# Retention values: copied from their bank at once, and scaled and turned two at a time

## The chip, the cores and the metric

The kernel runs on one core of a Trainium2 chip. The metric is the device time of one execution in microseconds (us), lower is better. The core has a matrix engine (TensorE, PE), a vector engine (VectorE, DVE), a scalar engine (ScalarE, ACT), GpSimd (POOL) and a queue that issues transfers (SyncE, SP). They run side by side and wait for one another only through semaphores. Matrix results land in PSUM, eight banks of 512 fp32 numbers per partition; a bank can be given to the next result when the last reader of the old one is through.

## The reference

The reference is one layer of a decoder: 512 tokens, width 1024, fp32. A normalised x is projected by one wide matrix to the inputs of two branches, a retention and a dilated attention, and to their two gates; the branches are merged and followed by an MLP and a gated embedding. The change concerns the retention alone. Its output y of head h (four heads, 256 wide) is found in four chunks of 128 tokens, then normalised over the 256 columns, gated and projected:

```python
y = retention_chunkwise(rq, rk, rv)
y = rmsnorm(y, ret_gn.reshape(RET_HEADS, RET_DV)).reshape(B, S, RET_V)
ret_branch = (jax.nn.silu(rg) * y) @ w_ret_out
```

With y the 128x256 result of one chunk and one head (called a value below), what is needed of it is the mean of its squares per token, the power -1/2 of that, the product of y, this factor and the gate G, and the transpose of the product, since the next matrix product wants columns.

## The kernel before, in words

All large products run on PE with each fp32 operand split in a high and a low part, three matmuls each (lines 260 to 262). A weight tile of 128x1024 is loaded (raw), its high part is copied out by ACT (whi, line 248) and its low part is the difference taken by DVE (wlo, line 249). Six raw tiles and four pairs of split tiles exist, so ACT and DVE work a few tiles ahead of PE and wait for PE to free them. Some weight tiles are sums of others: POOL issues transfers that add to a tile (line 226), and DVE adds tiles (line 224).

The heads have little work and are strewn into the large products. `later` puts a step on a list with a lag, and `tick`, called after every few matmuls of a product, takes steps off the list when their lag is over. Steps thus get their place in the written program from ticks; the framework's scheduler then sets the order of each engine's instructions. Each engine works its own queue strictly in that order.

The retention works in two pairs of heads. For each pair, a product of seven parts (`seven_products`, numbered m in the code) makes the pair's v and G. The steps of the pair's two heads (`ret_head`) are put on the list after that and run inside the next large product: those of heads 0 and 1 inside the product for v and G of heads 2 and 3, those of heads 2 and 3 inside the first of two gate products (`gates`, called in `mix`). The steps of a head are: scores (rs, line 978; masked by DVE to rsT, line 981), three states (kv, line 986; the first copied by ACT, line 989, the others summed by DVE to st, line 991), and four values (ry, lines 998 and 1000).

A value before the change goes this way. ACT takes its squares with their sum (line 1002). DVE makes the mean from the sum (v, line 325, in `rstd`), POOL takes the power (r, line 326), and DVE multiplies the bank's content by r and G into the tile At (line 1004). Three ticks later PE turns At in two transposes into another bank (pt, line 1010), and ACT copies the two halves with the norm's gains into A (line 1013). Steps up to line 1004 are written in one piece.

All small results, rs, kv, ry and pt, take their bank from one pool of four; part 2 of a seven-part product holds two of these four (pa) from its first half to its second. The second head of a pair runs in that time, so its scores, states and values share the other two. With G come its own DVE steps (lines 957, 959) and a sigmoid on ACT (line 958); with a gate product come sums and products on DVE (g, lines 1043 and 1045) and a sigmoid (line 1058). The framework gives a bank's next tile to the place that comes free first, so that the scores of the second head get the bank of the first head's third value, and the state behind them that of its fourth.

Of the kernel before, what the change touches and what calls it, by code (L numbers as in the profile page):

```python
# [13 lines left out]
AF = mybir.ActivationFunctionType  # L14
ALU = mybir.AluOpType
AX = mybir.AxisListType

P = 128
S = 512
D = 1024  # L20
NT = S // P
# [59 lines left out]
class Block:  # L81
# [292 lines left out]
    def turn(self, x, out, goff):  # L374

        ps = self.bank("pt")
        for k in range(4):
            self.nc.tensor.transpose(ps[:, k * P : (k + 1) * P], x[:, k * P : (k + 1) * P], self.ident)
        g = self.gcol[:, goff : goff + 4].unsqueeze(2).to_broadcast([P, 4, P])
        self.nc.vector.tensor_tensor(out, ps.rearrange("p (k t) -> p k t", k=4), g, op=ALU.mult)  # L380
# [586 lines left out]
    def ret_head(self, h, qk, v, G, inner, eps, A):  # L967
        nc = self.nc
        qT, kT, kd = qk
        c = slice((h % 2) * 256, (h % 2) * 256 + 256)  # L970
        hs = slice(h * HD, (h + 1) * HD)
        sT, st = [], []

        def scores():
            sc = self.bank("rs")
            for n in range(NT):
                i = slice(n * P, (n + 1) * P)
                nc.tensor.matmul(sc[:, i], kT[:, h, i], qT[:, h, i], start=True, stop=True)
            t = self.tmp("rsT")
            v4 = lambda ap: ap.rearrange("p (n i) -> p n i", n=NT)  # L980
            nc.vector.tensor_tensor(v4(t), v4(sc), inner.unsqueeze(1).to_broadcast([P, NT, P]), op=ALU.mult)
            sT.append(t)

        def state(n):
            ps = self.bank("kv")[:, :256]
            nc.tensor.matmul(ps, kd[:, n, hs], v[:, n, c], start=True, stop=True)
            s = self.tmp("st")[:, :256]
            if n == 0:
                nc.scalar.activation(s, ps, AF.Copy)
            else:  # L990
                nc.vector.tensor_tensor(s, st[-1], ps, op=ALU.add)
            st.append(s)

        def values(i):
            y = self.bank("ry")[:, :256]
            ss = self.small(1, "ss")
            r = slice(i * P, (i + 1) * P)
            nc.tensor.matmul(y, sT[0][:, r], v[:, i, c], start=True, stop=i == 0)
            if i:
                nc.tensor.matmul(y, qT[:, h, r], st[i - 1], start=False, stop=True)  # L1000
            At = self.tmp("At")
            nc.scalar.activation(At[:, 256:], y, AF.Square, accum_out=ss)
            r = self.rstd(ss, 1, 256, eps[:, i, h : h + 1])
            nc.vector.scalar_tensor_tensor(At[:, :256], y, r, G[:, i, c], op0=ALU.mult, op1=ALU.mult)
            self.later(3, lambda: turn(At, i), ("A", h, i))

        def turn(At, i):
            ps = self.bank("pt")
            for k in range(2):
                nc.tensor.transpose(ps[:, k * P : (k + 1) * P], At[:, k * P : (k + 1) * P], self.ident)  # L1010
            for k in range(2):
                g = self.gcol[:, 8 + 2 * h + k : 9 + 2 * h + k]
                nc.scalar.activation(A[h // 2][:, 2 * (h % 2) + k, i * P : (i + 1) * P], ps[:, k * P : (k + 1) * P],
                                     AF.Copy, scale=g)

        self.later(0, scores)
        for n in range(NT - 1):
            self.later(0, lambda n=n: state(n))
        for i in range(NT):
            self.later(2, lambda i=i: values(i))  # L1020
# [31 lines left out]
    def mix(self, A, O):  # L1052
        nc = self.nc
# [8 lines left out]

        self.gates(16, spill, "cb")
        for h in range(H):
            for i in range(NT):
                self.force(("A", h, i))
        O = self.merged_split(O)
        G = [self.big("Ga") for _ in range(2)]
        part = lambda kk: G[kk % 4 // 2][:, kk % 2 + kk // 4 * 2]
# [344 lines left out]
```

## Time and profile before

| | before |
| --- | --- |
| median of 3 runs | 968.77 us (967.72 to 969.59) |
| profiled execution, its own time | 968.49 us |
| its span, first to last instruction | 966.7 us |
| granted clock of PE | 1.00 |
| PE busy | 956.3 us, 5404 instructions |
| DVE busy | 721.1 us, 1029 instructions |
| ACT busy | 533.3 us, 1027 instructions |
| POOL busy | 146.4 us, 136 instructions |

In a timeline row stand start, duration, engine, line, operation, what is written from what, shapes, the number of merged instructions, and in brackets how long the engine was idle before it and what ended that. In a row of a group, the numbers behind the bar are busy us, mean ns of one, and idle us before them with what ended most of it. PEld are the weight loads of PE, which run beside its matmuls. The time of one execution is some 1.8 us more than the span. The two pairs of heads run between 330 and 440 us.

### The profile page before, as it was taken

How to read it: one execution, taken by the hardware profiler on the slowest of the kernel's cores; microseconds unless marked ns; L12 is line 12 of the kernel's file. 1: busy time of each engine (PE TensorE's matmuls, PEld its weight loads, DVE VectorE, ACT ScalarE, POOL GpSimd, SP SyncE). 2: the span in 40 equal slices, each digit the busy share in tenths (PEclk: the TensorE clock that was granted, in tenths of full speed). 3: DMA queues.
4: the chain of work that ended last, by engine and by line, in shares of the span. 5: the costliest groups of instructions: out<-in, count | busy, mean ns of one | idle time of the engine just before them, and what ended most of it. 6: DMA issues, size and time to landing. Idle time of an engine off the chain costs nothing.

```text
span 966.7 us, 14352 instructions
## 1 busy us (share of the span) xinstructions
PE 956.3 (99%) x5404; PEld 843.1 (87%) x5404; DVE 721.1 (75%) x1029; ACT 533.3 (55%) x1027; POOL 146.4 (15%) x136
## 2 busy tenths in 40 slices
PE   9999999999999999999999999999999999999998
PEld 6888899889888878899988888998998998898886
DVE  7857665775969957476856879799589679769953
ACT  6535344546636646467713445893585476468551
POOL 0310220210001021313002210211202202111100
PEclk9999999999999999999999999999999999999999
DMA  9832123234348564759757686968959868886911
GB/s 335 264 99 73 61 87 87 66 105 154 105 110 204 172 126 131 132 152 222 209 177 218 153 184 185 213 156 211 190 164 199 196 179 158 224 187 150 276 64 55
DMA packets 87189, 155.50 MB, mean 161 GB/s; under 512 B 6816, under 2 KB 18768, under 8 KB 87120
## 3 DMA queue, kind: packets, MB, share of 16 engines
q1 hardware_dynamic: 66304, 114.72, 36.4%
q0 software_dynamic: 20672, 39.85, 24.8%
q8 instruction: 42, 0.69, 0.3%
q14 instruction: 27, 0.22, 0.1%
q10 hardware_dynamic: 144, 0.02, 0.0%
HBM read 148.24 MB, written 6.33 MB: 160 GB/s over the span
## 4 chain that ended last, share of the span: by engine, by line
PE 90%; issue 4%; DVE 3%; POOL 2%; DMA 1%; ACT 1%; SPq 0%; POOLq 0%; DVEq 0%; ACTq 0%
PE pg L260 26%; PE pg L261 26%; PE pg L262 25%; PE pa L262 2%; PE pa L261 2%; PE pa L260 2%; PE po L734 1%; PE ph L587 1%; POOL r L326 1%; DVE wlo L249 1%; PE sc L711 1%; PE pe L679 1%; POOL raw L226 1%; DMA raw<-in_w_down 1%; PE sc L717 1%
## 5 line engine op out<-in xcount | busy, mean ns | idle before, releaser
L249 DVE TENSOR_TENSOR wlo<-raw,whi 128x1024 fp32r<-128x1024 f32 (+1 forms) x246 | 292.5, 1197 | 111.8 <-ACT whi L248 110.6
L248 ACT ACTIVATE whi<-raw 128x1024 fp32r<-128x1024 f32 (+1 forms) x245 | 253.4, 1039 | 213.0 <-PE pg L262 99.4
L260 PE MATMUL pg<-whi,hh 128*128 128x512 f32 x344 | 137.8, 402 | 0.0
L262 PE MATMUL pg<-whi,hl 128*128 128x512 f32 x344 | 134.7, 391 | 0.0
L261 PE MATMUL pg<-wlo,hh 128*128 128x512 f32 x344 | 134.5, 391 | 0.0
L260 PE MATMUL pg<-f,whi 128*128 128x256 f32 x384 | 108.9, 284 | 0.5 <-DVE r L1222 0.5
L261 PE MATMUL pg<-f,whi 128*128 128x256 f32 x384 | 108.7, 283 | 0.0
L262 PE MATMUL pg<-f,wlo 128*128 128x256 f32 x384 | 108.6, 283 | 0.0
L262 PEld LDWEIGHTS pg<-whi,hl 128*128 128x128 f32 x344 | 72.4, 210 | 11.2
L260 PEld LDWEIGHTS pg<-whi,hh 128*128 128x128 f32 x344 | 72.4, 211 | 10.4 <-ACT whi L248 0.3
L261 PEld LDWEIGHTS pg<-wlo,hh 128*128 128x128 f32 x344 | 72.6, 211 | 10.0
L260 PE MATMUL pg<-whi,f 128*128 128x512 f32 x192 | 75.4, 393 | 0.0
L261 PE MATMUL pg<-wlo,f 128*128 128x512 f32 x192 | 74.8, 390 | 0.0
L262 PE MATMUL pg<-whi,f 128*128 128x512 f32 x192 | 74.8, 389 | 0.0
L260 PEld LDWEIGHTS pg<-f,whi 128*128 128x128 f32 x384 | 73.7, 192 | 1.0 <-ACT r L1224 0.7
L261 PEld LDWEIGHTS pg<-f,whi 128*128 128x128 f32 x384 | 73.7, 192 | 0.2
L262 PEld LDWEIGHTS pg<-f,wlo 128*128 128x128 f32 x384 | 73.7, 192 | 0.0
L642 POOL TENSOR_TENSOR r<-v,mhalf 128x4 f32<-128x4 f32 x24 | 30.0, 1253 | 153.5 <-DVE v L641 150.6
L226 POOL DMA_DIRECT2D raw<-in_w_down x24 | 29.0, 1216 | 141.1 <-DVE wlo L249 112.4
L226 POOL DMA_DIRECT2D raw<-in_w_in x20 | 24.4, 1218 | 170.0 <-DVE wlo L249 157.6
L226 POOL DMA_DIRECT2D raw<-in_w_up x24 | 29.0, 1210 | 134.4 <-DVE wlo L249 129.1
L260 PEld LDWEIGHTS pg<-whi,f 128*128 128x128 f32 x192 | 36.1, 188 | 8.1 <-issue 0.4
(274 smaller groups left out, 2186.3 us busy)
## 6 DMA issues: line engine op xcount, KB each, us to landing
raw<-in_w_in SPq DMA_DIRECT2D x72, 512.0 KB, 3.9
raw<-in_w_up SPq DMA_DIRECT2D x32, 512.0 KB, 4.7
raw<-in_w_down SPq DMA_DIRECT2D x32, 512.0 KB, 4.7
raw<-in_w_up POOLq DMA_DIRECT2D x24, 512.0 KB, 7.5
raw<-in_w_down POOLq DMA_DIRECT2D x24, 512.0 KB, 6.1
raw<-in_w_in POOLq DMA_DIRECT2D x20, 512.0 KB, 6.4
x<-in_x SPq DMA_DIRECT2D x8, 512.0 KB, 8.3
raw<-in_w_ret_out SPq DMA_DIRECT2D x8, 512.0 KB, 4.1
```

What stands on the lines that cost most here:

```text
L226: self.nc.gpsimd.dma_start(raw, self.chained[i].rearrange("(k p) n -> p k n", p=P), accum_op=ALU.add)
L248: self.pin(nc.scalar.activation(R(hi[:, i]), raw[:, i], AF.Copy))
L249: nc.vector.tensor_tensor(R(lo[:, i]), raw[:, i], hi[:, i], op=ALU.subtract)
L260: t.matmul(ps, sh, mh, start=first, stop=False, skip_group_check=more)
L261: t.matmul(ps, sh, ml, start=False, stop=False, skip_group_check=more)
L262: t.matmul(ps, sl, mh, start=False, stop=last, skip_group_check=more)
L326: self.nc.gpsimd.tensor_tensor(r, v, self.mhalf[:, :w], op=ALU.pow)
L587: self.nc.tensor.transpose(ps[:, t * P : (t + 1) * P], rots[t][:, h * HD : (h + 1) * HD], self.ident)
L642: nc.gpsimd.tensor_tensor(r, v, self.mhalf[:, :H], op=ALU.pow)
L679: self.nc.tensor.transpose(ps[:, k * P : (k + 1) * P], e[:, k * P : (k + 1) * P], self.ident)
L711: nc.tensor.matmul(sc[:, h * P : (h + 1) * P], qT[:, h, rs], kT[:, h, rs], start=True, stop=True)
L717: nc.tensor.matmul(sc[:, h * 256 : (h + 1) * 256], qT[:, 2 * hp + h, rs], kT[:, 2 * hp + h, (r - 1) * P : (r + 1) * P], start=True, stop=True)
```

## The change

A value leaves its bank by ACT alone: a copy to At, then the squares, written back into the bank, with their sum. Two values share one At (256 columns each) and one small tile each for sums, means and powers. When the second of the two is there, `means` makes both means in one DVE instruction and both powers in one POOL instruction; `scale`, two ticks later, multiplies each half of At in place by its power and by G on DVE; `turn`, three ticks later, turns both values by four transposes into one bank, and ACT copies them to A in two instructions of 128x256. What waits for A at the end of `mix` asks for two keys per head instead of four.

```diff
         def values(i):
             y = self.bank("ry")[:, :256]
...
-            At = self.tmp("At")
-            nc.scalar.activation(At[:, 256:], y, AF.Square, accum_out=ss)
-            r = self.rstd(ss, 1, 256, eps[:, i, h : h + 1])
-            nc.vector.scalar_tensor_tensor(At[:, :256], y, r, G[:, i, c], op0=ALU.mult, op1=ALU.mult)
-            self.later(3, lambda: turn(At, i), ("A", h, i))
-
-        def turn(At, i):
+            n, m = i // 2, i % 2
+            if not m:
+                pair[n] = self.tmp("At"), self.small(2, "ss"), self.small(2, "v"), self.small(2, "r")
+            At, ss = pair[n][:2]
+            nc.scalar.activation(At[:, 256 * m : 256 * (m + 1)], y, AF.Copy)
+            nc.scalar.activation(y, y, AF.Square, accum_out=ss[:, m : m + 1])
+            if m:
+                self.later(1, lambda: means(n))
+
+        def means(n):
+            _, ss, u, r = pair[n]
+            nc.vector.scalar_tensor_tensor(u, ss, 1.0 / 256, eps[:, 2 * n : 2 * n + 2, h], op0=ALU.mult, op1=ALU.add)
+            nc.gpsimd.tensor_tensor(r, u, self.mhalf[:, :2], op=ALU.pow)
+            self.later(2, lambda: scale(n))
+
+        def scale(n):
+            At, r = pair[n][0], pair[n][3]
+            for m in range(2):
+                y = At[:, 256 * m : 256 * (m + 1)]
+                nc.vector.scalar_tensor_tensor(y, y, r[:, m : m + 1], G[:, 2 * n + m, c], op0=ALU.mult, op1=ALU.mult)
+            self.later(3, lambda: turn(n), ("A", h, n))
+
+        def turn(n):
+            At = pair.pop(n)[0]
             ps = self.bank("pt")
+            for k in range(4):
+                nc.tensor.transpose(ps[:, k * P : (k + 1) * P], At[:, k * P : (k + 1) * P], self.ident)
+            pv = ps.rearrange("p (i k t) -> p k i t", i=2, k=2)
             for k in range(2):
-                nc.tensor.transpose(ps[:, k * P : (k + 1) * P], At[:, k * P : (k + 1) * P], self.ident)
...
+                kk = 2 * h + k
+                out = A[h // 2][:, kk % 4, 256 * n : 256 * (n + 1)].rearrange("p (i t) -> p i t", i=2)
+                nc.scalar.activation(out, pv[:, k], AF.Copy, scale=self.gcol[:, 8 + kk : 9 + kk])
```

What it moves shows in the order of the instructions, and only between the first and the last of the heads' own. On PE, at the scores of the first pair's second head (pa and pg are banks of the large product, hh and hl the split x, us a split sum of it), before:

```order
L261 MATMUL pa_3326<-wlo_3227,hh_144 128x512
L262 MATMUL pa_3326<-whi_3226,hl_146 128x512
L260 MATMUL pg_3202<-whi_3269,us_2069 128x512
L978 MATMUL rs_3333<-qT_2278,hT_2814 128x128 x4
L986 MATMUL kv_3340<-v_3073,kd_2275 128x256
L261 MATMUL pg_3202<-wlo_3270,us_2069 128x512
```

and now:

```order
L261 MATMUL pa_3310<-wlo_3227,hh_144 128x512
L262 MATMUL pa_3310<-whi_3226,hl_146 128x512
L978 MATMUL rs_3317<-qT_2278,hT_2814 128x128 x4
L986 MATMUL kv_3324<-v_3073,kd_2275 128x256
L260 MATMUL pg_3202<-whi_3261,us_2069 128x512
L261 MATMUL pg_3202<-wlo_3262,us_2069 128x512
```

The scores stand one weight matmul earlier. In the second pair their place is the old one.

On PE, at the second pair's turnings, which before began inside the second half of part 2 of the gate product (pa):

```order
L260 MATMUL pa_3834<-hh_144,whi_3951 128x256
L1010 MATMUL pt_4044<-ident,At_3750 128x128 x2
L261 MATMUL pa_3834<-hl_146,whi_3951 128x256
L262 MATMUL pa_3834<-hh_144,wlo_3952 128x256
L1010 MATMUL pt_4087<-ident,At_3796 128x128 x2
L260 MATMUL pg_3623<-us_2067,whi_4001 128x256
L1010 MATMUL pt_4092<-ident,At_3807 128x128 x2
L261 MATMUL pg_3623<-us_2067,whi_4001 128x256
```

and now stand in the middle and at the end of the product's last part:

```order
L261 MATMUL pg_3595<-hl_146,whi_4029 128x256
L262 MATMUL pg_3595<-hh_144,wlo_4030 128x256
L1028 MATMUL pt_4146<-ident,At_3710 128x128 x4
L1028 MATMUL pt_4153<-ident,At_3759 128x128 x4
L260 MATMUL pg_3596<-hh_144,whi_4025 128x256
L261 MATMUL pg_3596<-hl_146,whi_4025 128x256
```

The transposes come eight at a time, some 80 weight matmuls later than the first of them did.

On DVE, towards the end of the second pair, before (g and v are the gates and the means, L325 a mean, L1004 a scaling):

```order
L1043 TENSOR_TENSOR g_3912<-g_3912,pg_3623 128x512
L1043 TENSOR_TENSOR g_3926<-g_3926,pg_3624 128x512
L325 TENSOR_SCALAR v_3985<-ss_3980,dec 128x1
L1045 TENSOR_TENSOR g_3912<-g_3912,r_free 128x512
L1004 SCALAR_TENSOR_TENSOR At_3983<-ry_3979,r_3986,G_3461 128x256
L325 TENSOR_SCALAR v_3996<-ss_3991,dec 128x1
L1045 TENSOR_TENSOR g_3926<-g_3926,r_free 128x512
L1004 SCALAR_TENSOR_TENSOR At_3994<-ry_3990,r_3997,G_3461 128x256
L1043 TENSOR_TENSOR g_3682<-g_3682,pa_3821 128x512
```

and now (L1013 a mean, L1021 a scaling), up to the first two splits for the next gate product:

```order
L1013 SCALAR_TENSOR_TENSOR v_3932<-ss_3931,dec 128x2
L249 TENSOR_TENSOR wlo_4030<-raw_3534,whi_4029 128x1024
L1062 TENSOR_TENSOR g_3740<-g_3740,pg_3595 128x512
L1021 SCALAR_TENSOR_TENSOR At_3710<-At_3710,r_3713,G_3429 128x256
L1064 TENSOR_TENSOR g_3740<-g_3740,r_free 128x512
L1021 SCALAR_TENSOR_TENSOR At_3759<-At_3759,r_3762,G_3429 128x256 x2
L1062 TENSOR_TENSOR g_3754<-g_3754,pg_3596 128x512
L1021 SCALAR_TENSOR_TENSOR At_3886<-At_3886,r_3889,G_3429 128x256
L1064 TENSOR_TENSOR g_3754<-g_3754,r_free 128x512
L1021 SCALAR_TENSOR_TENSOR At_3886<-At_3886,r_3889,G_3429 128x256
L1021 SCALAR_TENSOR_TENSOR At_3930<-At_3930,r_3933,G_3429 128x256 x2
L249 TENSOR_TENSOR wlo_4102<-raw_4099,whi_4101 128x1024
```

Scalings of both heads, which before were spread over the whole time of the pair, stand together ahead of the next product's weight splits. On POOL, a pair's four powers stand next to one another, with no transfer issue between them.

More of the change, by code (lines that the diff above doesn't have):

```diff
@@ L992, in state @@
             st.append(s)
+        pair = {}
         def values(i):
             y = self.bank("ry")[:, :256]
-            ss = self.small(1, "ss")
             r = slice(i * P, (i + 1) * P)
@@ L1009, in turn @@
             for k in range(2):
[L1010 to L1014, printed above, removed]
+                kk = 2 * h + k
+                out = A[h // 2][:, kk % 4, 256 * n : 256 * (n + 1)].rearrange("p (i t) -> p i t", i=2)
@@ L1064, in mix @@
         for h in range(H):
-            for i in range(NT):
-                self.force(("A", h, i))
+            for n in range(2):
+                self.force(("A", h, n))
         O = self.merged_split(O)
```

## The prediction, made before the changed kernel was run

> **What bounds the kernel now.** The page comes first: TensorE (PE) is busy for all but about 10 us of the span, so work taken from another engine is worth nothing in itself, and a gain can only come from places where PE stands.
>
> ```profile
> span 966.7 us, 14352 instructions
> PE 956.3 (99%) x5404; PEld 843.1 (87%) x5404; DVE 721.1 (75%) x1029; ACT 533.3 (55%) x1027; POOL 146.4 (15%) x136
> ```
>
> Next I asked who makes PE wait between 325 and 445 us, the stretch in which the four retention heads run.
>
> ```profile
> PE rs L978 <- DVE At L1004: 2.3, 2, 1.4
> PE ry L998 <- DVE At L1004: 0.5, 1, 0.5
> PE pt L1010 <- DVE At L1004: 0.3, 1, 0.3
> ```
>
> Each row gives total, times and longest, in us. All three name one releaser: the scaling of a value (At, line 1004) on VectorE (DVE). The first two are waits for a PSUM bank: the scores of a pair's second head (rs) and one later value (ry) need a bank from which an older value has not yet been read for the last time. The third is a wait for the value that is to be turned. No row of PE names a weight (whi, wlo) there.
>
> These idle times understate the loss, since a matmul's modelled end lies beyond the start of its successor. So I went to PE's timeline and took starts. Weight matmuls of 512 columns start every 0.23 us here and those of 256 every 0.12 us; an undisturbed scores block of a pair's first head is the measure for the two disturbed ones.
>
> ```profile
> 333.89 0.39 PE L262 MATMUL pg<-whi,hl 128*128 128x512 f32 x1
> 334.12 1.05 PE L978 MATMUL rs<-qT,hT 128*128 128x128 f32 x8
> 335.25 0.59 PE L260 MATMUL pg<-whi,us 128*128 128x512 f32 x1
> ...
> 350.34 0.39 PE L260 MATMUL pg<-whi,us 128*128 128x512 f32 x1
> 351.64 1.16 PE L978 MATMUL rs<-qT,hT 128*128 128x128 f32 x8 [0.91 <-DVE At L1004]
> 353.26 0.58 PE L261 MATMUL pg<-wlo,us 128*128 128x512 f32 x1
> ...
> 403.59 0.28 PE L262 MATMUL pa<-hh,wlo 128*128 128x256 f32 x1
> 405.22 1.16 PE L978 MATMUL rs<-qT,hT 128*128 128x128 f32 x8 [1.35 <-DVE At L1004]
> 406.90 0.47 PE L260 MATMUL pg<-us,whi 128*128 128x256 f32 x1
> ```
>
> From the weight matmul ahead of the block to the one behind it: undisturbed 335.25 - 333.89 = 1.36 us. Second head of the first pair: 353.26 - 350.34 = 2.92, so 1.56 us lost. Second head of the second pair: 406.90 - 403.59 = 3.31 against 1.36 - 0.11 = 1.25 (its preceding matmul is a 256-column one), so 2.06 us lost.
>
> ```profile
> 363.44 0.39 PE L262 MATMUL pg<-whi,us 128*128 128x512 f32 x1
> 363.94 0.70 PE L998 MATMUL ry<-v,rsT 128*128 128x256 f32 x2
> ...
> 421.73 0.28 PE L261 MATMUL pa<-hl,whi 128*128 128x256 f32 x1
> 422.50 0.70 PE L998 MATMUL ry<-v,rsT 128*128 128x256 f32 x2 [0.49 <-DVE At L1004]
> ...
> 425.02 0.28 PE L260 MATMUL pa<-hh,whi 128*128 128x256 f32 x1
> 428.35 0.29 PE L260 MATMUL pg<-us,whi 128*128 128x256 f32 x1
> ```
>
> The two late values: 0.50 where 0.23 is usual plus a first pair that is 0.11 longer than an undisturbed one's 0.59 is 0.38 us; 0.77 where 0.12 is usual plus the same 0.11 is 0.76 us. From 425.02 to 428.35 PE starts 12 weight matmuls (1.44) and four turnings of two transposes (8 x 0.11, 0.88): 2.32 of 3.33, so 1.01 us lost around the turnings. Together 1.56 + 2.06 + 0.38 + 0.76 + 1.01 = **5.8 us** in which PE stands in this stretch, all of it behind the scaling.
>
> Why is the scaling so late? The timelines of ScalarE (ACT), DVE and GpSimd (POOL) show it for the third value, whose bank the scores at 351.64 wait for.
>
> ```profile
> 347.52 0.38 ACT L1002 ACTIVATE At<-ry 128x256 f32<-128x256 f32 x1
> 349.33 0.21 DVE L325 TENSOR_SCALAR v<-ss,dec 128x1 f32<-128x1 f32 x1
> 349.45 1.22 DVE L224 TENSOR_TENSOR raw<-raw,raw 128x1024 f32<-128x1024 f32 x1
> 349.62 1.46 POOL L326 TENSOR_TENSOR r<-v,mhalf 128x1 f32<-128x1 f32 x1 [1.85 <-DVE v L325]
> 351.11 0.48 DVE L1004 SCALAR_TENSOR_TENSOR At<-ry,r,G 128x256 f32<-128x256 f32 x1 [0.44 <-POOL r L326]
> ```
>
> The squares are taken by 347.90, but the mean waits in DVE's queue behind weight work until 349.33, the power takes POOL until 351.08, and the scaling ends the bank's use at 351.59. PE starts the scores at 351.64. So of the 4.1 us from the squares' start to the release 3.7 are a detour over two engines and back.
>
> **The change part by part.** *Copy and squares.* A value now leaves its bank by a copy on ACT and the squares behind it, with no other engine between. What each costs:
>
> ```profile
> L989 ACT ACTIVATE st<-kv 128x256 f32<-128x256 f32 x4 | 1.5, 385 | 5.0 <-PE kv L986 5.0
> L1002 ACT ACTIVATE At<-ry 128x256 f32<-128x256 f32 x16 | 6.1, 381 | 2.6 <-DVE G L957 1.7 <-PE ry L998 0.6 <-PE ry L1000 0.2
> L1002 ACT ACTIVATION_READ_ACCUMULATOR At<-ry 128x1 f32 x16 | 3.2, 199 | 0.0
> L1013 ACT ACTIVATE A<-pt,gcol 128x128 f32<-128x128 f32 x32 | 9.3, 368 | 2.1 <-PE pt L1010 2.1
> L248 ACT ACTIVATE whi<-raw 128x1024 fp32r<-128x1024 f32 x33 | 34.7, 1059 | 27.9 <-PE pg L261 10.9 <-issue 7.9 <-PE pg L262 7.8
> ```
>
> The state's copy (line 989) has the new copy's very shape, 128x256 from PSUM: 0.385 us, 16 of them, 6.2 us of ACT. Is it in time? In the first pair:
>
> ```profile
> 346.58 1.05 ACT L248 ACTIVATE whi<-raw 128x1024 fp32r<-128x1024 f32 x1
> 347.18 0.59 PE L1000 MATMUL ry<-st,qT 128*128 128x256 f32 x2
> ```
>
> ACT is through with a weight copy at 347.63, about when PE ends the fourth value (347.77). Copy, squares and sum for the third and fourth value then take 2 x (0.385 + 0.381 + 0.199) = 1.93 us even end to end: done by 349.6, the third already by 348.6. The scores now stand one matmul earlier, where PE is at 350.34; the state behind them, later by the scores' length, needs the fourth value's bank. So 1.7 us are to spare for the scores, and more than 0.7 for the state: I take both scores stalls as gone. Between the ends stand 0 regained (ACT 3 us later than worked out) and all of 1.56 + 2.06. The two late values need the first and second value's banks, freed by the same two ACT instructions while 12 weight matmuls run: 0.38 + 0.76 gone as well.
>
> *Means and powers for two values at once.* Sixteen means and sixteen powers become eight each:
>
> ```profile
> L325 DVE TENSOR_SCALAR v<-ss,dec 128x1 f32<-128x1 f32 x16 | 3.3, 207 | 2.2 <-ACT At L1002 2.2
> L1004 DVE SCALAR_TENSOR_TENSOR At<-ry,r,G 128x256 f32<-128x256 f32 x16 | 7.7, 483 | 12.3 <-POOL r L326 12.2
> ```
>
> At 0.207 us that takes 1.7 us off DVE, and POOL is no longer ahead of any bank: no gain on PE by itself. The scaling keeps its size but reads SBUF twice. No row shows that form at 256 columns; a quarter of the 1.22 us addition above gives 0.31, that plus the 0.207 of a smallest instruction 0.51. I keep 0.48, since the old form lies between. The 12.2 us that DVE stood for powers is cover: nobody waits for the scaling now but the turning, which is moved behind it.
>
> Here a row and a rule meet. The power above took 1.46 us beside the addition of two SBUF tiles and ended 0.4 us after it; the next one ran alone:
>
> ```profile
> 351.79 0.54 POOL L326 TENSOR_TENSOR r<-v,mhalf 128x1 f32<-128x1 f32 x1 [0.72 <-DVE v L325]
> ```
>
> The Trainium skill, "SBUF — State Buffer", section "Who interferes with whom", says that a DVE instruction with two SBUF inputs contends with a GpSimd instruction that reads SBUF; the trace agrees (1.46 against 0.54 us). It speaks against this change, which turns the scaling into such an instruction. By the rows a power beside a scaling may come 0.48 us later; four in a pair are 1.9 us of DVE's slack, not of PE's time, so the sum is the same with it and without.
>
> *Turning.* As many transposes as before, 32 of 0.11 us, now eight in a row at four places where two or four stood: no change of PE work. They stand in the last product of a pair, long behind the first head's scalings. The 1.01 us around them should go; ends 0 and 1.01, I take all. Their copies on ACT, 32 of 0.368 us (11.8), become 16, taken at the 0.385 of the 128x256 copy (6.2): with the 6.2 of new copies ACT is 0.6 us fuller, which the 27.9 us that it stood ahead of weight copies hide; without them ACT would be late by that 0.6 us.
>
> *DVE at a pair's end* is the cover that could go. All eight scalings of the second pair now stand ahead of the next gate's first weight split, where three stood.
>
> ```profile
> 425.00:440.00 15.00, 14.65 (x120) 14.03 (x119) 14.51 (x20) 14.31 (x34) 0.95 (x2) 1.00 0.65 197
> ...
> 434.10 1.22 DVE L249 TENSOR_TENSOR wlo<-raw,whi 128x1024 fp32r<-128x1024 f32 x1
> ...
> 440.60 0.28 PE L262 MATMUL pg<-hh,wlo 128*128 128x256 f32 x1
> ```
>
> DVE is busy 14.51 of 15 us there. That split ends at 435.32 and PE first uses it at 440.60: a lead of 5.3 us. Five more scalings take 5 x 0.48 = 2.4, PE comes 0.76 + 1.01 = 1.8 earlier, and with the three old scalings go three waits for powers, 0.44 us each as at 351.11: 5.3 - 2.4 - 1.8 + 1.3 = 2.4 us of lead left. So nothing is lost, but with less in hand.
>
> **Sum.** 5.8 us won, less 0.4 that I allow for small new waits (the size of the least of the old ones, 0.38): 5.4. Against the profiled execution, span 966.7 and own time 968.49, that is 963.1; the median of the three runs, 968.77, lies 0.28 above that execution, so **963.4**. About 0.2% (1.9 us) is what a measurement of this kernel can tell from no change.
>
> **The rivals.** *ACT is late (part of the gain).* A weight copy of 1.05 us that waits for its buffer stands between the values' copies in three of the four heads. If each bank wait keeps half (half of 4.8 us), or one scores stall and the turnings stay, 2 to 4 us are won: 964.8 to 966.8. For it: one copy more per value in a queue in order. Against: the 0.7 to 1.7 us worked out. Chance 0.19.
>
> *Nothing comes of it.* PE is early and then stands for weights instead, so the 5.8 us return: 967 to 969.5. For it: the transfers right behind the heads.
>
> ```profile
> 430.00:470.00 40.00, 40.00 (x336) 40.00 (x335) 29.39 (x32) 28.63 (x45) 7.26 (x6) 1.00 0.91 224
> ```
>
> The DMA engines are busy 0.91 of that time. Against: PE is busy 40.00 of 40.00 all the same, and buffers come free by PE's own pace. Chance 0.06.
>
> *Slower: DVE stands for powers at a pair's end.* The first scaling of two values may find its power not ready:
>
> ```profile
> 347.80 0.48 DVE L1004 SCALAR_TENSOR_TENSOR At<-ry,r,G 128x256 f32<-128x256 f32 x1 [2.10 <-POOL r L326]
> ```
>
> If DVE stands 2.1 us for each of a pair's four powers, that is 8.4 us ahead of the splits, 6.0 beyond the lead of 2.4; in both pairs 12.0 lost against 5.8 won, 975.0. It makes the kernel slower from 5.3 us of such waits a pair on. Against it: means and scalings now stand apart in the order, and that row's power was behind a DMA issue on POOL, of which none stands between the powers now. Chance 0.10. With the 1.9 us of the contention above taken from the lead, 0.5 us of it stays, and the point falls to 3.4 us a pair: without that I would have given 0.07.
>
> **How the numbers follow.** The forecast has 0.65 and its own range is 962.2 to 964.8 (all 5.8 gone, 963.0, and 0.8 for the runs' spread, the lowest of which lies 1.05 below the median; to 4 us won). For 8 in 10 the range reaches into the first rival: 962.0 to 966.8. Faster: 0.65 + 0.19 = 0.84; same 0.06; slower 0.10.
>
> **What would show it.** Right: no wait of PE for At or for ry's banks in the waits between 325 and 445 us, scores blocks of 1.36 and 1.25 us, PE idle in that stretch under 0.5 us. Wrong: scores that wait for ACT's squares (first rival), PE or its loads waiting for wlo or whi at a pair's end, with DVE standing for r (third), or raw landing late (second).

## The result, and the profile after

| | before | after |
| --- | --- | --- |
| median of the timed runs | 969.18 us (967.72 to 969.94, without one execution of 1181.73) | 962.09 us (961.47 to 963.72) |
| ratio after to before | | 0.9933, 95% interval 0.9920 to 0.9947 |
| profiled execution, its own time | 968.49 us | 961.97 us |
| its span | 966.7 us | 960.2 us |

The change makes the kernel faster by 5.1 to 7.8 us (969 us times one minus the ends of the interval). 963.4 us was forecast, with a range from 962.0 to 966.8: the gain is there, and it is larger than forecast. The median lies only 0.09 us above the lower end of that range, and 0.1 us below the forecast's own range of 962.2 to 964.8. The page of the profile after begins so:

```profile
span 960.2 us, 14325 instructions
PE 953.5 (99%) x5404; PEld 843.3 (88%) x5404; DVE 718.3 (75%) x1021; ACT 534.5 (56%) x1027; POOL 143.5 (15%) x128
```

The work is the same to a few instructions (16 fewer on VectorE and GpSimd together). What changed is when PE stands. The waits of PE over the whole span of after (total, times, longest, in us):

```profile
PE warm L436 <- DVE warm L432: 1.4, 1, 1.4
PE pg L490 <- DVE whi L244: 0.9, 1, 0.9
```

Both are of the first 6 us. The three rows of the prediction that named the scaling between 325 and 445 us have no successor, nor has a fourth of the same view, which the prediction did not show (its time is within the 2.06 us counted there for the second pair's scores):

```profile
PE kv L986 <- DVE At L1004: 0.2, 1, 0.2
```

The windows of the heads say the same (length, then busy us of PE, PEld, DVE, ACT, POOL, clock, DMA share, GB/s), first before, then after:

```profile
330.00:380.00 50.00, 48.86 (x229) 39.89 (x229) 35.86 (x52) 28.83 (x58) 10.19 (x12) 1.00 0.54 126
380.00:440.00 60.00, 57.63 (x424) 54.60 (x424) 37.90 (x56) 35.87 (x75) 13.35 (x14) 1.00 0.67 155
```

```profile
330.00:380.00 50.00, 50.00 (x235) 42.02 (x234) 34.58 (x48) 30.06 (x58) 7.84 (x8) 1.00 0.55 126
380.00:440.00 60.00, 60.00 (x468) 58.62 (x467) 40.23 (x55) 40.57 (x82) 15.18 (x12) 1.00 0.73 174
```

PE has no idle time left there, and in the same 110 us it gets through 703 instructions instead of 653. Its timeline shows the two scores blocks that stood:

```profile
334.45 1.05 PE L978 MATMUL rs<-qT,hT 128*128 128x128 f32 x8
...
350.44 0.39 PE L262 MATMUL pa<-whi,hl 128*128 128x512 f32 x1
350.67 1.05 PE L978 MATMUL rs<-qT,hT 128*128 128x128 f32 x8
351.56 0.60 PE L986 MATMUL kv<-v,kd 128*128 128x256 f32 x2
351.81 0.59 PE L260 MATMUL pg<-whi,us 128*128 128x512 f32 x1
...
401.72 0.28 PE L262 MATMUL pa<-hh,wlo 128*128 128x256 f32 x1
401.84 1.06 PE L978 MATMUL rs<-qT,hT 128*128 128x128 f32 x8
...
402.98 0.47 PE L260 MATMUL pg<-us,whi 128*128 128x256 f32 x1
...
566.13 0.60 PE L378 MATMUL pt<-ident,x 128*128 128x128 f32 x4
```

From the weight matmul ahead to the one behind, 351.81 - 350.44 = 1.37 us and 402.98 - 401.72 = 1.26, where 1.36 and 1.25 were forecast.

**A measure for what follows.** Spans of single executions differ by over 1 us for reasons that have nothing to do with the heads (below). So I take a stretch of PE that holds all of the heads and little else that can stand: from the start of the first scores to the first transpose of x at the merge (line 378). In every kernel here 1374 instructions of PE start in it. The row that ends it in before (its first scores start at 334.12, in the prediction) is

```profile
571.84 0.60 PE L378 MATMUL pt<-ident,x 128*128 128x128 f32 x4
```

Before: 571.84 - 334.12 = 237.72 us. After: 566.13 - 334.45 = **231.68**. The heads give 6.04 us. The span's difference of 6.5 is that, less 0.33 that after started its first scores later, plus 0.8 behind the stretch.

ScalarE's timeline at the third and fourth value of the first pair's first head, where the prediction worked out 1.93 us for copies, squares and sums:

```profile
347.85 0.38 ACT L1006 ACTIVATE At<-ry 128x256 f32<-128x256 f32 x1
348.11 0.39 ACT L1007 ACTIVATE ry<-ry 128x256 f32<-128x256 f32 x1
348.42 0.20 ACT L1007 ACTIVATION_READ_ACCUMULATOR ry<-ry 128x1 f32 x1
348.50 0.38 ACT L1006 ACTIVATE At<-ry 128x256 f32<-128x256 f32 x1
348.77 0.39 ACT L1007 ACTIVATE ry<-ry 128x256 f32<-128x256 f32 x1
349.07 0.20 ACT L1007 ACTIVATION_READ_ACCUMULATOR ry<-ry 128x1 f32 x1
```

It took 1.42 us (347.85 to 349.27), since each instruction starts some 0.1 us before the one ahead has ended. The third bank is free at 348.62, 2.0 us before the scores; the fourth at 349.27, 2.3 us before the state. The groups of the changed instructions between 325 and 440 us:

```profile
L1014 POOL TENSOR_TENSOR r<-v,mhalf 128x2 f32<-128x2 f32 x8 | 8.5, 1071 | 32.0 <-DVE v L1013 31.9
L1021 DVE SCALAR_TENSOR_TENSOR At<-At,r,G 128x256 f32<-128x256 f32 x16 | 7.2, 478 | 0.8 <-POOL r L1014 0.8
L1033 ACT ACTIVATE A<-pt,gcol 128x256 f32<-128x256 f32 x16 | 6.3, 484 | 0.5 <-PE pt L1028 0.5
```

The scaling of SBUF costs 0.478 us, as much as that of the bank before (0.483), and VectorE stands 0.8 us for powers where it stood 12.2.

### The profile page after: what moved, and what is told of

Read it like the earlier page. It is cut to its first block, busy times and chain, and to the rows that moved or that the text cites. A ratio compares the mean times of both kernels' runs of the same rounds, so it can differ in the third digit from the quotient of the medians.

```text
span 960.2 us, 14325 instructions
## 1 busy us (share of the span) xinstructions
PE 953.5 (99%) x5404; PEld 843.3 (88%) x5404; DVE 718.3 (75%) x1021; ACT 534.5 (56%) x1027; POOL 143.5 (15%) x128
## 4 chain that ended last, share of the span: by engine, by line
PE 98%; DVE 1%; DMA 0%; ACT 0%; issue 0%; SPq 0%; DVEq 0%
PE pg L260 27%; PE pg L261 27%; PE pg L262 27%; PE pa L262 3%; PE pa L261 3%; PE pa L260 3%; PE po L734 1%; PE ph L587 1%; PE sc L711 1%; PE ry L999 1%; PE pe L679 1%; PE kv L986 1%; PE sc L717 1%; PE ry L1001 1%; DMA raw<-in_w_in 0%; PE rs L978 0%
```

## The experiments

Two theories were set against each other. *Bank theory*: the gain comes from the banks that ScalarE frees early. *Pairing theory*: it comes from half the means and powers, and from turnings that are grouped and later. Each run lists its median and its ratio to runs of the kernel before on the same chip; the stretch comes from its own profile.

| kernel | median us | ratio (95%) | stretch us |
| --- | --- | --- | --- |
| before | 968.6 to 969.2 | 1 | 237.72 |
| copy alone | 965.11 | 0.9963 (0.9951 to 0.9974) | 234.33 |
| pairs alone, banks held | 967.10 | 0.9985 (0.9976 to 0.9994) | 235.78 |
| copy and grouped turnings | 963.74 | 0.9944 (0.9930 to 0.9957) | 232.69 |
| the same and shared means and powers (one step) | 963.68 | 0.9948 (0.9935 to 0.9961) | 231.99 |
| the change, again | 962.74 | 0.9936 (0.9924 to 0.9949) | 231.68 |
| squares taken from the copy | 963.61 | 0.9942 (0.9930 to 0.9954) | 231.68 |
| before, turning later | 968.72 | 1.0000 (0.9989 to 1.0011) | 237.66 |
| copy alone, turning later | 965.86 | 0.9969 (0.9959 to 0.9980) | 233.70 |
| 12 more copies of the third value | 963.35 | 0.9945 (0.9932 to 0.9958) | 231.90 |
| 8 more copies of third and fourth value | 963.67 | 0.9942 (0.9930 to 0.9955) | 232.56 |
| 4 more scalings | 961.95 | 0.9928 (0.9916 to 0.9941) | 231.68 |
| 16 more scalings | 966.03 | 0.9973 (0.9963 to 0.9982) | 236.09 |

**The copy alone.** Kernel before, with

```diff
-            nc.scalar.activation(At[:, 256:], y, AF.Square, accum_out=ss)
+            nc.scalar.activation(At[:, :256], y, AF.Copy)
+            nc.scalar.activation(y, y, AF.Square, accum_out=ss)
             r = self.rstd(ss, 1, 256, eps[:, i, h : h + 1])
-            nc.vector.scalar_tensor_tensor(At[:, :256], y, r, G[:, i, c], ...)
+            nc.vector.scalar_tensor_tensor(At[:, :256], At[:, :256], r, G[:, i, c], ...)
```

> The kernel before with one edit: each value is copied by ScalarE out of its bank and squared there, and the scaling then works in SBUF. Means, powers and turnings stay single and where they were. Bank theory (the gain comes from banks that ScalarE frees without a detour over VectorE and GpSimd): PE no longer waits for rs and ry banks, 4.8 us are won; the turnings still stand three ticks behind the scaling, so up to 1.0 us of standing around them may stay. 962 to 964.5 us. Pairing theory (the gain comes from half the means and powers and from turnings that are grouped and later): 967.5 to 969.5, no gain.

Measured: 965.11 us, between the two. Its timeline of PE: the ends of the stretch, and a scores block without any stall.

```profile
334.97 1.05 PE L978 MATMUL rs<-qT,hT 128*128 128x128 f32 x8
...
351.19 1.05 PE L978 MATMUL rs<-qT,hT 128*128 128x128 f32 x8
...
371.15 0.95 PE L1011 MATMUL pt<-ident,At 128*128 128x128 f32 x4
...
569.30 0.60 PE L378 MATMUL pt<-ident,x 128*128 128x128 f32 x4
```

The stretch is 234.33, 3.39 us won: both scores stalls (3.62) are gone, as the bank theory says. But something has taken their place. The waits of PE's weight loads (which run ahead of the matmuls and show a wait sooner) between 325 and 445 us:

```profile
PEld pt L1011 <- ACT A L1014: 1.7, 4, 0.6
PEld ry L998 <- ACT ry L1003: 0.7, 2, 0.4
PEld pg L260 <- DVE g L1044: 0.4, 1, 0.4
```

The turnings now stand for banks that ScalarE is copying to A (line 1014), two late values for a bank whose squares came late, and a part of the gate product for a bank that VectorE has not yet read (g, line 1044). From PE's starts, as in the prediction, 0.55 and 0.87 us are lost at two turnings (PE at 371.15 and 424.19), 0.47 at the product's bank behind a third one (431.17) and 0.58 at the two late values: 2.5 of the 2.65 us by which this stretch is longer than that of the change. The wait of the late values is the first rival in small: a weight copy that waits for its buffer stands ahead of a value's copy in ScalarE's queue.

```profile
363.16 1.06 ACT L248 ACTIVATE whi<-raw 128x1024 fp32r<-128x1024 f32 x1 [1.83 <-PE pg L262]
364.12 0.37 ACT L1002 ACTIVATE At<-ry 128x256 f32<-128x256 f32 x1
```

So neither theory holds alone.

**Pairs alone.** The changed kernel without its copy, means and scalings in one piece, the scaling reading two banks:

```diff
-            nc.scalar.activation(At[:, 256 * m : 256 * (m + 1)], y, AF.Copy)
-            nc.scalar.activation(y, y, AF.Square, accum_out=ss[:, m : m + 1])
+            nc.scalar.activation(At[:, 256 * m : 256 * (m + 1)], y, AF.Square, accum_out=ss[:, m : m + 1])
+            held.append(y)
...
-                nc.vector.scalar_tensor_tensor(y, y, r[:, m : m + 1], ...)
+                nc.vector.scalar_tensor_tensor(y, held.pop(0), r[:, m : m + 1], ...)
```

> The changed kernel with its first half undone: two values share mean, power and four transposes as in the change, but there is no copy; the scaling reads both values from their banks as in the kernel before, in one piece behind the second value. Pairing theory: most of the gain stays, 962 to 965 us. Bank theory: the first value of two holds its bank until the second is there and the shared power is done, so PE stands at least as long as before for rs, kv and ry banks: 968.5 us or more, up to 975.

Measured: 967.10 us, a small gain that neither theory expected. Its waits of PE between 325 and 445 us:

```profile
PE rs L978 <- DVE At L1021: 1.1, 2, 0.7
PE ry L999 <- DVE At L1021: 0.6, 1, 0.6
PE pt L1028 <- DVE At L1021: 0.5, 2, 0.3
PE pa L260 <- DVE At L1021: 0.3, 1, 0.3
```

The waits for banks stay, as the bank theory says, but those of the scores are half of before's 2.3 us: one power instead of two stands ahead of the last scaling of two values. That this outweighs the first bank's longer hold is argued, not shown. The stretch is 1.94 us shorter than before.

**Grouped turnings on top of the copy.** Two values in one At, turned by four transposes into one bank and copied by two instructions; means, powers and scalings single:

```diff
...
-            nc.scalar.activation(y, y, AF.Square, accum_out=ss[:, m : m + 1])
+            ss = self.small(1, "ss")
+            nc.scalar.activation(y, y, AF.Square, accum_out=ss)
+            r = self.rstd(ss, 1, 256, eps[:, i, h : h + 1])
+            Am = At[:, 256 * m : 256 * (m + 1)]
+            nc.vector.scalar_tensor_tensor(Am, Am, r, G[:, i, c], op0=ALU.mult, op1=ALU.mult)
             if m:
-                self.later(1, lambda: means(n))
...
+                self.later(3, lambda: turn(n), ("A", h, n))
```

(The functions `means` and `scale` go.)

> The kernel with the copy alone, and the two values of a tile turned together (four transposes in one bank, two copies on ScalarE); means, powers and scalings stay single, in one piece behind each value. If what the copy alone left (2.7 us) was a matter of turnings that each want a bank and two copies of ScalarE: nearly all of it goes, 962 to 963.5 us. If it was the number of means and powers on VectorE and GpSimd: it stays, 964 to 965.5.

Measured: 963.74 us, stretch 232.69: 1.64 us of what the copy alone left goes with the grouping, and the median lies between the two ranges. Of the 1.64 us, 0.58 are the two late values, which stand close to each other here and no longer wait, 0.47 are the wait for the product's bank, and only 0.45 lie at the turnings themselves: 1.42 us were lost there, and 0.97 still are (from the weight matmul ahead of the turnings, 370.68, to the second one behind, 372.99, are 2.31 us, where 0.23 + 8 x 0.11 + 0.23 = 1.34 are usual). Whether fewer banks or fewer copies did it, no run tells apart. One wait of PE is left in the heads, again for ScalarE's copies out of a turning's bank:

```profile
PE pt L1019 <- ACT A L1024: 0.5, 1, 0.5
```

**One step.** The changed kernel with means and scalings straight behind the second value (`later` around them taken out).

> The changed kernel without steps of their own: means, powers and both scalings stand straight behind the second of two values; copies, pairs and groups of four transposes stay. Bank theory with steps that matter little: the banks are as early as in the change; VectorE stands for eight powers at up to 0.76 us each (the mean of the 16 before), 3 us a pair against a lead of 3.4, so 962 to 963.5 us. Steps theory (the turnings' stall goes only since scalings and turnings stand apart): the 1.9 us around the turnings that the copy alone left stay, 963.5 to 965.

Measured: 963.68 us, stretch 231.99. Shared means and powers are worth 0.70 us more, and the steps of their own only the last 0.31. The median lies in the range of the steps theory; the stretch speaks against it, since 0.31 stay and not 1.9. The 0.70 us are all at the turning where the grouped kernel still stood: from 370.59 to 372.18, between the same two matmuls, are 1.59 us here, 0.25 over the usual, where it was 0.97. ScalarE's copies out of the banks of the turnings ahead start 0.8 us sooner, first the grouped kernel, then this one:

```profile
370.67 1.55 ACT L1024 ACTIVATE A<-pt,gcol 128x256 f32<-128x256 f32 x4
```

```profile
369.85 1.54 ACT L1033 ACTIVATE A<-pt,gcol 128x256 f32<-128x256 f32 x4
```

In the grouped kernel the sigmoid that stands ahead of them in ScalarE's queue waits 0.86 us for a sum by VectorE (line 957), and VectorE had just stood 0.44 us for a single value's power. Here that sigmoid does not wait. So a power that is late can still hold up PE, by way of the sigmoid and the copies. VectorE, however, stands for the powers again (between 325 and 445 us):

```profile
DVE At L1021 <- POOL r L1014: 8.8, 7, 2.3
```

These are 8.8 us, 4.4 in a pair, against 0.8 in the change. That is the condition of the rival that forecast a slower kernel (3.4 to 5.3 us a pair), nearly in full, and it cost PE 0.31 us: the waits are spread over the pair and do not all fall ahead of its end.

**Turning later.** Two kernels, before and the copy alone, with a lag of 9 for 3:

```diff
-            self.later(3, lambda: turn(At, i), ("A", h, i))
+            self.later(9, lambda: turn(At, i), ("A", h, i))
```

> The kernel before with one edit: the turning of a value is put nine ticks behind its scaling instead of three, so the transposes stand about 12 weight matmuls later in the second pair. Bank theory: only the 1.0 us around the turnings can be won, the waits for banks stay: 967.7 to 969 us. Pairing theory (later turnings are what counts): 963 to 966 us.

> The kernel with the copy alone, and the turning nine ticks behind instead of three; means, powers, scalings and turnings stay single. If the 1.9 us that stayed around its turnings are a matter of their place: they go in the second pair, where the transposes move by 12 weight matmuls (1.3 us of them), 963.3 to 964.5 us. If they come from single turnings (a bank and two copies on ScalarE for each): nothing changes, 964.5 to 965.5.

Measured: 968.72 us, as the bank theory has it, and 965.86, above both ranges; the stretches are 0.06 and 0.63 us shorter. These runs settle less than I had expected of them. The lag moves only the turnings of a pair's second head; those of the first head, at which PE stood, keep their place with either lag. On the kernel before, what stood there stays. On the copy alone the first pair's stall goes from 0.55 to 0.43 us, the second pair's 0.87 goes altogether although that turning has not moved, and the wait for the product's bank grows from 0.47 to 0.82. Why the 0.87 goes is not shown, and place alone is left untested.

**Squares from the copy.** The changed kernel with `At` for `y` as what is squared: the bank is free after the copy.

> The changed kernel with one edit: the squares are taken from the copy in SBUF, so the bank is free after the copy alone, some 0.3 us sooner. Bank theory: the copy with the squares in the bank was early enough by 1.9 us at the scores, so nothing changes: within 0.5 us of 962.1. If ScalarE were still the one that PE waits for (first rival): 0.3 us at each of some eight places, 960 us or less.

Measured: the stretch is 231.68 us, the same to 0.01; the median is 1.5 us above that of the change beside before and 0.9 above its repetition, and the intervals of the ratios overlap. So the median misses the 0.5 us that were expected, while the stretch, which alone looks at the heads, does not move. Freeing banks still sooner brings nothing.

**Holding banks longer.** The copy repeated, for the third value of each pair's first head (13 times), and for third and fourth (9 times each).

> The changed kernel with twelve more copies of the third value of each pair's first head, all from its bank, so ScalarE holds that bank 3.2 us (0.27 from start to start, as copy and squares follow each other) to 4.6 us (0.385 end to end) longer. Bank theory: the scores of the second head, for which ScalarE was early by 1.9 us in the first pair and 2.3 in the second, now stand by the rest, 0.9 to 2.7 us in each pair: 964 to 967.5 us, and PE waits for rs behind ScalarE. Pairing theory (banks don't matter, and ScalarE has 40% of idle time): 962 us.

> The changed kernel with eight more copies of the third and of the fourth value of each pair's first head, out of their banks; in the run with twelve more of the third alone the scores took the fourth value's bank, which came free first. With 16 copies of 0.27 to 0.41 us (five that write one tile took 2.04 there) both banks are held 4.3 to 6.6 us longer; the scores now stand ten weight matmuls (2.3 us) later in the first pair, with 1.9 us in hand. Bank theory: PE stands for rs behind ScalarE 0.1 to 2.4 us in each pair, and the states behind it: 963 to 967.5 us. Pairing theory: no wait for rs, 962 to 963.5.

Measured: stretches of 231.90 and 232.56 us, 0.22 and 0.88 us longer; the medians, 963.35 and 963.67, can hardly be told from the 962.09 and 962.74 of the change. The first missed its aim: the scores take whichever bank comes free first, which was the fourth value's, and its time lies below what was expected. The second shows the wait that the bank theory wants (PE, 325 to 445 us, and ScalarE's copies ahead of it):

```profile
PE rs L978 <- ACT ry L1008: 0.2, 1, 0.2
```

```profile
347.86 4.82 ACT L1007 ACTIVATE At<-ry 128x256 f32<-128x256 f32 x17
352.44 0.52 ACT L1008 ACTIVATE ry<-ry 128x256 f32<-128x256 f32 x1
```

16 copies of 0.284 us are 4.5 us more ahead of the release, and the scores of the first pair were also put ten matmuls (2.3 us) later. By the change's own rows the bank is then free at 348.62 + 4.54 = 353.16 and PE is there at 350.67 + 2.28 = 352.95; the scores start at 353.10. PE's weight loads wait in this way in both pairs, 0.4 us each. So ScalarE's time in hand is real, and it ends where the rows put it.

**More work for VectorE at a pair's end.** The change with scalings into a tile that nobody reads, 16 in the second pair, or 4 in the last head:

```diff
+                if h > 1:
+                    junk = self.tmp("jk")
+                    for _ in range(2):
+                        nc.vector.scalar_tensor_tensor(junk[:, :256], y, r[:, m : m + 1], ...)
```

> The changed kernel with two more scalings, into a tile that nobody reads, behind each of the eight scalings of the second pair: 16 x 0.4 to 0.48 = 6.4 to 7.7 us of VectorE ahead of the next gate's first weight splits, which were 3.4 us early. Lead theory: PE stands there by the rest, 3.0 to 4.3 us: 965 to 967 us. If VectorE has slack that the order doesn't show: 962 to 963.5.

> The same with one more scaling behind each of the four of the last head: 1.6 to 1.9 us, less than the lead of 3.4 us. Lead theory: nothing stands, 962 to 963.5 us. If the changed kernel had no VectorE time in hand there: 964 to 965.

Measured: 966.03 us with 16, stretch 4.41 us longer; 961.95 with 4, stretch 231.68. In the change itself the first split of the next gate ends at 430.34 + 1.22 = 431.56, and PE first uses it at 434.91, a lead of 3.35 us (VectorE's and PE's timelines):

```profile
430.34 1.22 DVE L249 TENSOR_TENSOR wlo<-raw,whi 128x1024 fp32r<-128x1024 f32 x1
...
434.91 0.28 PE L262 MATMUL pg<-hh,wlo 128*128 128x256 f32 x1
```

With 16 scalings more that matmul comes at 437.72, and what follows it is told under the hardware below: 1.5 of the 4.41 us are a lower clock, and the 2.9 that remain lie just under the 3.0 to 4.3 expected.

**The change once more**, unaltered, for what stands outside the heads.

> The changed kernel once more, unaltered, beside the three that follow: 961.5 to 963.7 us, PE standing about 0.2 us in all around the heads' blocks. What PE stands behind line 1202 or 1241 between 600 and 900 us should differ from the first profile of this kernel if it is a matter of when transfers land (0.1 us there, up to 2.8 us in the four experiments so far), and be the same 0.1 us if the change removed it.

Measured: 962.74 us, stretch 231.68 again. But PE's and VectorE's waits between 600 and 900 us, where nothing of the change runs, are not those of the first profile of the same program (there PE has no such row, and VectorE's says 4.6, 4, 1.4):

```profile
PE pg L260 <- DVE r L1241: 0.9, 3, 0.4
```

```profile
DVE raw L224 <- DMA raw<-in_w_down: 5.8, 4, 1.8
```

VectorE's queue stands for a weight transfer, and PE for what VectorE has behind it. This differs from execution to execution of one program: what lies behind the stretch takes 394.1 us in the first profile (960.2 - 566.13) and 395.7 in this one (961.5 - 565.84). Before's profile had 394.9 and such a wait of 0.5 us at 712 us; that after had none was chance, not the change.

## Why the prediction was right, and where not

*The scores.* Both stalls, 1.56 and 2.06 us, were put down to a bank that the scaling had not yet read, and were to go with a release by ScalarE alone. With the copy alone they are gone. Right in cause and size.

*The late values.* Their 1.14 us were to go by the same release. With the copy alone half of it, 0.58, stays as a wait for ScalarE's squares, which is the mechanism of the first rival. It goes only in the kernels with grouped turnings, where the two values stand side by side.

*ScalarE in time.* 1.7 us for the scores and over 0.7 for the state were worked out; 2.0 and 2.3 are there, since copy, squares and sum overlap at their edges (0.65 us for a value, not 0.965). The copy of a turning is the other way off: 0.484 us where 0.385 was taken from the state's copy, whose gain is no pointer and whose source lies in one piece; whether that is the reason was not tested. Nothing hung on it.

*The turnings.* This is the step that failed: the 5.8 us were said to be "all of it behind the scaling", and the 1.01 us around the turnings were to go because the turning is "moved behind it". The total came out, the cause did not, and that much of the hit is luck. With the copy alone the scaling holds no bank any more, and PE stands longer at the turnings than before: 1.42 us, and 0.47 at a bank of the product behind them. The turnings stand for banks and for ScalarE: a bank and two copies for each value, while another product holds two of the four banks. One row of before's groups had said so, and I had read only the matmuls' row beside it (the weight loads of the turnings, 325 to 445 us: three releasers, and the copies to A are the largest):

```profile
L1010 PEld LDWEIGHTS pt<-ident,At 128*128 128x128 f32 x32 | 3.7, 141 | 1.9 <-ACT A L1013 0.7 <-DVE At L1004 0.5 <-DVE g L1043 0.2
```

Grouping the turnings, with 8 banks and 16 copies for 16 values instead of 16 and 32, takes 0.45 of the 1.42 us and the 0.47; the rest goes with shared powers and with the steps of their own. "No change of PE work", as the prediction has it, is true, and it passed over that this halves the claims on what PE waits for.

*Means and powers.* They were put down as "no gain on PE by itself". On top of copy and grouping they bring 0.70 us, since VectorE is sooner with the sums that ScalarE's queue waits for ahead of its copies.

*The shares.* By the stretch the change is 3.39 us of copy, 1.64 of grouped turnings, 0.70 of shared means and powers and 0.31 of steps of their own, 6.04 in all. The order in which they are added matters: pairs alone, on the kernel before, bring 1.94.

*The size.* 5.8 us were found in before's timeline and 0.4 of them allowed for new small waits; 6.04 were there, and no new wait came: four kernels have the stretch at 231.68 to the hundredth. The missing 0.24 were not traced in full; some 0.1 are small losses at the first pair's turnings, which I had not added up. The allowance was not needed. Together that is 0.64 us; the rest of the 1.3 us between forecast and median lies within the spread of what stands behind the heads.

*VectorE.* The lead at the end of the second pair was to shrink from 5.3 to 2.4 us; it is 3.35, and the two doses of scalings put its end where it should be: 1.6 to 1.9 us more cost nothing, 6.4 to 7.7 more cost 4.41, of which 2.9 are the wait and what hangs on it and 1.5 the clock.

A power beside a scaling was to come 0.48 us later; that does not show. Of the eight powers of the changed kernel, each of two columns, one takes 0.72 us with VectorE idle, four take 0.69 to 0.84 beside scalings, and three 1.54 to 1.62 beside an addition or a split of 1024 columns; these make the mean of 1.07. The first of these rows has scalings beside it, the second an addition (line 224):

```profile
367.63 0.81 POOL L1014 TENSOR_TENSOR r<-v,mhalf 128x2 f32<-128x2 f32 x1 [0.26 <-DVE v L1013]
```

```profile
416.50 1.62 POOL L1014 TENSOR_TENSOR r<-v,mhalf 128x2 f32<-128x2 f32 x1 [10.18 <-DVE v L1013]
```

The Trainium skill, "SBUF — State Buffer", section "Who interferes with whom", has an instruction of VectorE with two SBUF inputs contend with one of GpSimd that reads SBUF, as the prediction told for the scalings; the trace agrees at the additions and splits, not at the scalings (0.69 to 0.84 us against 0.72). VectorE is not the only thing that makes a power longer: three of the one-step kernel take 1.2 us while VectorE is idle. Late powers cost 0.8 us of VectorE and nothing of PE, since means and scalings stand apart.

*The rivals.* ScalarE late: not in the change, though the copy alone shows it in small. Nothing: refuted, PE is busy 110.00 of 110 us. Slower through powers: its condition was made in the one-step kernel, and it cost 0.31 us, because the 8.4 us were taken to fall all ahead of the pair's end.

## What to carry to other kernels

When an instruction in order waits for a PSUM bank, look at every engine that the last read of that bank passes through, and let the one that is nearest and least busy take the data out at once; the arithmetic can follow in SBUF. Then count the banks and the copies that the steps behind it claim, since they are the next to be waited for: here grouping them was worth 1.64 of 6.04 us, part of it through other waits that went with them. And measure such a change over a stretch of the bounding engine with a fixed number of instructions: it gave 231.68 us four times over, while spans of the same kernels differed by up to 1.9 us.

## What the runs showed of the hardware

PE's clock can fall after a wait of 2.3 us. In the profiled execution of the kernel with 16 more scalings PE stands once that long for a weight split, and it then runs at full speed for 1.4 us before its matmuls of 256 columns start every 0.21 us instead of every 0.12. Its timeline and two windows (the clock is the third number from the end):

```profile
437.72 0.39 PE L262 MATMUL pg<-hh,wlo 128*128 128x256 f32 x1 [2.28 <-DVE wlo L249]
...
439.53 0.41 PE L262 MATMUL pg<-hh,wlo 128*128 128x256 f32 x1
439.74 0.41 PE L260 MATMUL pg<-hh,whi 128*128 128x256 f32 x1
```

```profile
438.00:439.00 1.00, 1.00 (x10) 1.00 (x10) 1.00 (x2) 1.00 (x2) 0.00 (x0) 1.00 0.35 37
440.00:442.00 2.00, 2.00 (x11) 2.00 (x11) 2.00 (x3) 1.97 (x4) 0.00 (x0) 0.50 0.73 201
```

The clock is at half from 439.2 to 442.6 us, 3.4 us. From 439.14 to 442.67 PE starts 17 matmuls in 3.53 us, where 17 x 0.12 = 2.04 are usual, so 1.5 us are lost: the wait costs some two thirds as much again as it lasts. It need not do so every time. 3.4 us at half would bring the mean clock of an execution down by 0.002; of the nine timed executions of this kernel six have a mean of 0.997 to 0.999 and three one of 1.000. Waits of up to 1.35 us, as in the kernel before, left the clock at 1.00. The Trainium skill, "TensorE: Matmul & The Clock Gate", section "Part 1: The HAM clock gate (the "warmup" mystery)", has the clock halved after an idle window of about 3.4 us; the length of the slow phase agrees with that window, but here 2.3 us of idle time were enough. The rival that forecast 975.0 us had priced a stall of 6 us a pair at its length alone.
